# Block sums of an output weight spread over more slabs, and more weight buffers in the output projection, in a one-core hybrid decoder layer

## Chip, core and metric

One core of a Trainium2 chip. The metric is device time in microseconds (us) for one execution. The kernel before took 2124.35 us (median of three runs, 2124.03 to 2127.09); the execution that was profiled took 2120.17 us.

## What is computed

A decoder layer on x of 1024 tokens by 2048 channels, in float32:

```
h     = rms_norm(x, attn_norm_g)
proj  = h @ w_in                       # 7776 columns, split into the parts below
q,k,v = silu(causal_conv4(gq, gk, gv)) # 8 heads of 128: group A
o_a   = gated_delta_rule(q, k, v, g, beta);  o_a = rms_norm(o_a) * silu(gz)
I     = sum_h w[t,h] * relu(q_idx[t,h] . k_idx[s])   # indexer, 16 heads of 64
o_b   = softmax attention of each query over its 256 best keys by I, * silu(az)
out   = rms_norm(x + concat(o_a, o_b) @ w_out, final_norm_g)
```

## The kernel before

**Numbers.** Each float32 factor is split into a high part `hi` (rounded by a ScalarE copy) and a rest `lo`, and a product is three matmuls (hi·hi, hi·lo, lo·hi).

**Input projection.** The work is cut into slabs of 256 columns of `w_in`. A slab has 8 pieces (`w_piece`, L198): SyncE (SP) loads the piece into `wraw` (3 buffers, 256 KB), ScalarE (ACT) writes `whi` (L194), GpSimd (POOL) writes `wlo` (L195; 2 buffers each), and TensorE (PE) does 24 matmuls of 512 columns with it (L289). Order of the slabs: V of the attention, a small one, four slabs `iq` of the indexer and the fifth `qk` slab (beside them the indexer's scores, with loads `iqr` at L492), four `qk` slabs (beside them the search for the 256th best score on VectorE, DVE, L661), then `k` 0 to 3 and `q` 0 to 3 of group A with their convolutions (beside them the attention, whose queries are loaded as `qaT`, L810, and whose masks are stored at L690), `v` 0 to 3 (beside them a triangular solve on DVE), and the gates, with the delta rule beside them.

**Output projection.** One level of Strassen's scheme: seven products (i = 0 to 6) of 512 x 1024 x 1024, each as two halves c of 8 pieces k. Four of the seven right factors are sums of 1024 x 1024 blocks of `w_out`. These sums (`wsum`, 4 MB each, in DRAM) are formed by DMA alone: eight steps (copy a block, or add one to it with an accumulating DMA), each cut into 4 parts of R = 256 rows (1 MB), 32 DMAs from POOL's queue. `block_sums` (L1130) puts them into a list `per_piece`; `w_piece` takes one off the list in pieces 1 to 5 of each slab and issues it on POOL right behind that piece's `wlo`. The list holds 17 entries of the delta rule's decay first, so the first `wsum` DMA goes out in the fourth `qk` slab and the last in slab `q` 1.

A piece of the output (`w_out_piece`, L219) loads `wraw` (same 3 buffers), ACT writes `whi` (L228) and DVE writes `wlo` (L229); two pieces of three have their `whi`/`wlo` in pool `wp` (2 buffers), the third in pool `op` (1 buffer). PE does 12 matmuls with it (L1383). At the end of each half `take` (L1319) adds the four PSUM banks to accumulators on DVE, `with_x` (L1301) loads x into a tile `xr` of pool `stage` (4 buffers) and adds it on POOL, and `square` (L1309) has ACT sum the squares, with its unused elementwise output in a small bfloat16 tile `jk` of its own.

**What sets the order.** Every engine and queue works in order. The order is written by a list planner from priorities (weights first, then evictions, side work, matmuls) and a timeline that it simulates, so an instruction that waits holds up all behind it on its engine.

Of the kernel before, what the change touches and what calls it, by code (L numbers as in the profile page):

```python
# [12 lines left out]
F32 = mybir.dt.float32  # L13
F32R = mybir.dt.float32r
BF16 = mybir.dt.bfloat16
I32 = mybir.dt.int32
AF = mybir.ActivationFunctionType
ALU = mybir.AluOpType
# [4 lines left out]
P = 128  # L23
T = 1024
D = 2048
# [14 lines left out]
HT = 512  # L40
# [12 lines left out]
def hybrid_layer(ctx: ExitStack, tc, x, positions, attn_norm_g, w_in, conv_w, a_log, dt_bias,  # L53
                 gdn_g, w_out, final_g, out):
    nc = tc.nc
    V, S, G, PE, SP = nc.vector, nc.scalar, nc.gpsimd, nc.tensor, nc.sync
# [3 lines left out]
    w_out = w_out[0]  # L60
# [5 lines left out]
    @contextmanager  # L66
    def pri(base):
        if active[0] == base:
            yield
            return  # L70
        saved = tc.cur_priority, active[0]
        tc.cur_priority, active[0] = count.get(base, base), base
        yield
        count[base] = tc.cur_priority
        tc.cur_priority, active[0] = saved
# [5 lines left out]
    wp = ctx.enter_context(tc.tile_pool(name="wp", bufs=3))  # L81
    gp = ctx.enter_context(tc.tile_pool(name="gp", bufs=1))
    stage = ctx.enter_context(tc.tile_pool(name="stage", bufs=2, side="right"))
    dr = ctx.enter_context(tc.tile_pool(name="dr", bufs=1, space=DRAM))
# [42 lines left out]
    def after(ins, prev):  # L127

        tc.add_manual_dep(ins.ins, prev.ins.name,
                          mybir.DependencyInfo(mybir.DependencyClass.NoSync, mybir.DependencyReason.DATA), reason="order")  # L130
        return ins
# [57 lines left out]
    w0 = w0_cm.__enter__()  # L189

    per_piece = []

    def w_split(whi, wlo, raw, ncol, eng):
        ins = S.activation(whi[:, :, :ncol], raw[:, :, :ncol], AF.Copy)  # L194
        low = eng.tensor_tensor(wlo[:, :, :ncol], raw[:, :, :ncol], whi[:, :, :ncol].bitcast(F32), op=ALU.subtract)  # L195
        return ins, low

    def w_piece(srcs, p, ncol, w2d, keep=False, into=None):  # L198

        with pri(P_W):  # L200
            raw = wp.tile([P, KPP, CG], F32, tag="wraw", name="wraw")
            o = 0
            for c0, n in srcs:
                SP.dma_start(raw[:, :, o:o + n], w2d[p * KPP * P:(p + 1) * KPP * P, c0:c0 + n].rearrange("(k p) c -> p k c", p=P))
                o += n
            if into is not None:
                whi, wlo = into
            elif keep and p >= 2:
                whi = w0.tile([P, KPP, CG], F32R, name=f"whi0_{p}")
                wlo = w0.tile([P, KPP, CG], F32R, name=f"wlo0_{p}")  # L210
            else:
                whi = wp.tile([P, KPP, CG], F32R, tag="whi", name="whi", bufs=2)
                wlo = wp.tile([P, KPP, CG], F32R, tag="wlo", name="wlo", bufs=2)
            ins = w_split(whi, wlo, raw, ncol, G)
            if per_piece and 1 <= p <= 5:
                per_piece.pop(0)(*ins)
        return whi, wlo

    def w_out_piece(src):  # L219

        with pri(P_W):
            shape = [P, 2 * CG]
            raw = wp.tile(shape, F32, tag="wraw", name="wraw")
            SP.dma_start(raw, src)
            pool, bufs = (op, 1) if next(turn_k) % 3 == 2 else (wp, 2)
            whi = pool.tile(shape, F32R, tag="whi", name="whi", bufs=bufs)
            wlo = pool.tile(shape, F32R, tag="wlo", name="wlo", bufs=bufs)
            S.activation(whi, raw, AF.Copy)  # L228
            V.tensor_tensor(wlo, raw, whi.bitcast(F32), op=ALU.subtract)  # L229
        return whi, wlo  # L230
# [344 lines left out]
    with tc.tile_pool(name="dp", bufs=1, reuse_waits="tile") as dp, pri(P_SIDE):  # L575
# [3 lines left out]
        r = dp.tile([P, NB, HEADS], F32, name="drr")  # L579
# [30 lines left out]
    early_cm.__exit__(None, None, None)  # L610


    maskS = [dr.tile([P, (b + 1) * P], BF16, name=f"mask{b}") for b in range(NB)]
    with tc.tile_pool(name="scp", bufs=1, reuse_waits="tile") as scp:
        score = {b: scp.tile([P, (b + 1) * P], F32, name=f"score{b}") for b in range(2, NB)}
        with ExitStack() as ixs:
            ixk = ixs.enter_context(tc.tile_pool(name="ixk", bufs=1, reuse_waits="tile"))
            kst = [ixk.tile([P, T], F32R, name=f"kst{i}") for i in range(2)]
            wi = ixk.tile([P, NB, 16], F32, name="wi")
            with pri(P_SIDE):  # L620
                V.tensor_scalar(wi, sm[:, :, 0:16], 0.03125, None, op0=ALU.mult)
                with tc.tile_pool(name="ikp", bufs=1, reuse_waits="tile") as ikp:
                    raw = ikp.tile([P, T], F32, name="ikr")
                    for i in range(2):
                        SP.dma_start(raw[64 * i:64 * i + 64], ikT)
                    S.activation(kst[0], raw, AF.Copy)
                    V.tensor_tensor(kst[1], raw, kst[0].bitcast(F32), op=ALU.subtract)
            ixp = ixs.enter_context(tc.tile_pool(name="ixp", bufs=1, reuse_waits="tile"))

            for cslab in range(4):  # L630
                iq_slab(cslab)
            proj_qk(4, budget=float("inf"))
# [6 lines left out]
        with tc.tile_pool(name="tkp", bufs=1, reuse_waits="tile") as tkp, pri(P_SIDE):  # L639
# [40 lines left out]
            for i in reversed(range(NK)):  # L680
                b, n = blocks[i], (blocks[i] + 1) * P
# [247 lines left out]
    def part(c, q):  # L929
        return (q * NB + c) * HEADS  # L930
# [70 lines left out]
    def delta_rule(g2):  # L1001
        def t4(tag, bufs):
            return g2.tile([P, 4, P], F32, tag=tag, name=tag, bufs=bufs)
# [53 lines left out]
        def step(c, ld, St, last):  # L1057
            G2 = range(2)
            pa = [mm4("pa", ld[g]["kT"], St[g]) for g in G2]
            prepare(c, ld)  # L1060
            R = []
            for g in G2:
                R.append(t4("R", 2))
                for h in range(4):
                    V.scalar_tensor_tensor(R[g][:, h, :], pa[g][:, h, :], col(cg, c, g, h), ld[g]["vb"][:, h, :],
                                           op0=ALU.mult, op1=ALU.add)
            pv = [mm4("pv", ld[g]["TT"], R[g]) for g in G2]
            vn = []
# [50 lines left out]
            SP.dma_start(szT[:, i0 + g, h * HT:(h + 1) * HT], sz[:, 3:])  # L1119
        slab_cm([(c0, CG)], CG, ev, budget=budget)  # L1120


    HC = D // 2

    def wo(i, j):
        return w_out[(1 - i) * HC:(2 - i) * HC, j * HC:(j + 1) * HC]

    wsum = {n: dr.tile([HC, HC], F32, name=f"wsum{n}") for n in (1, 2, 3, 4)}

    def block_sums():  # L1130

        R = 256

        def part(dst, src, add, r):
            def fn(ins, low):
                sl = slice(r * R, (r + 1) * R)
                ld = G.dma_start(wsum[dst][sl], src[sl], accum_op=ALU.add) if add else G.dma_start(wsum[dst][sl], src[sl])
                after(ld, low)
            return fn
        for dst, src, add in ((1, wo(0, 0), False), (3, wo(0, 1), False), (1, wo(0, 1), True), (3, wo(1, 1), True),  # L1140
                              (2, wsum[1], False), (2, wo(1, 1), True), (4, wsum[2], False), (4, wo(1, 0), True)):
            for r in range(HC // R):
                per_piece.append(part(dst, src, add, r))

    def decay_units():

        E = {}
# [33 lines left out]
        proj_qk(c)  # L1181
    tabs_cm.__exit__(None, None, None)
    with tc.tile_pool(name="atp", bufs=1, reuse_waits="tile") as atp:
        block_sums()
        attention(atp, kvp)
        total = sum(w for w, _ in todo)
        slabs = [("k", i) for i in range(4)] + [("q", i) for i in range(4)]
        for n, (nm, i) in enumerate(slabs):
            proj_conv(nm, {"k": C_GK, "q": C_GQ}[nm] + i * CG, 2 * i,
                      budget=float("inf") if n == NSLAB - 1 else total / NSLAB)  # L1190
            if n == 4:
                with pri(P_SIDE):
                    V.tensor_scalar(ssk, ssk, 4 * EPS, None, op0=ALU.add)
                    rsqrt(gp, rk.rearrange("p b h -> p (b h)"), ssk.rearrange("p b h -> p (b h)"), NU)
                    V.tensor_tensor(vs, rk, beta, op=ALU.mult)
                    V.tensor_tensor(cg, cn, egc, op=ALU.mult)
                    V.tensor_scalar(vs, vs, 0.5, None, op0=ALU.mult)
# [32 lines left out]
    op = ctx.enter_context(tc.tile_pool(name="op", bufs=1, reuse_waits="tile"))  # L1230
    turn_k = itertools.count()
# [6 lines left out]
    pairs = [[bigt(f"pr{i}{q}", [P, NT, 2, HT], F32R) for q in range(2)] for i in range(2)]  # L1238
    acc = [bigt(f"acc{i}", [P, NT, HC]) for i in range(2)]
    y11 = bigt("y11", [P, NT, HC])  # L1240
    m22 = bigt("m22", [P, KH, HT])
# [59 lines left out]
    def with_x(hf, ch, j, cs, sub=False):  # L1301

        xr = stage.tile([P, 3 + HT], F32, tag="xr", name="ox", bufs=4)[:, 3:]
        t0 = hf * HT + j * P
        SP.dma_start(xr, x[t0:t0 + P, ch * HC + cs.start:ch * HC + cs.stop])
        y = ys[hf, ch][:, j, cs]
        G.tensor_tensor(y, y, xr, op=ALU.subtract if sub else ALU.add)

    def square(hf, ch, j, c):  # L1309
        cs = slice(c * 512, (c + 1) * 512)  # L1310
        jk = op.tile([P, 512], BF16, tag="jk", name="jk", bufs=1)
        n = 2 * ch + c
        S.activation(jk, ys[hf, ch][:, j, cs], AF.Square, accum_out=ss[:, NT * hf + j, n:n + 1])

# [132 lines left out]
```

## Time and profile before

| | |
|---|---|
| median of the runs | 2124.35 us |
| profiled execution | 2120.17 us, span 2118.5 us |
| PE busy | 2030.4 us (96%) |
| DVE / ACT / POOL busy | 1350.0 / 882.0 / 685.2 us |
| mean granted clock of TensorE | 0.991 |
| DMA bytes | 285.59 MB, mean 135 GB/s |

Busy times are sums over a span; PE busy close to the span means that the kernel's time is PE's work plus the gaps in it. The granted clock is 1.00 where the full 2.4 GHz is granted; lower values in a stretch mean that part of it ran at 1.2 GHz.

### The profile page before, as it was taken

The page shows a single profiled execution, that of the slowest core. Times are in us where ns is not written, and L with a number is a line of the kernel's source. Part 1 is how long each engine was busy: PE and PEld are TensorE (multiplying, and loading weights), DVE is VectorE, ACT ScalarE, POOL GpSimd, SP SyncE. Part 2 cuts the span into 40 slices and gives each one's busy share as a digit, 9 for nine tenths or more (in the row PEclk, how much of TensorE's full clock was granted, in tenths as well). Part 3 has the DMA queues.
Part 4 walks back from the last instruction along what each step waited for, and adds up shares of the span by engine and source line. Part 5 has one row for each costly group of instructions (what it writes and reads, how often), then busy time and mean ns, then how long its engine had stood idle before and what let it go on. Part 6 is the DMA issues. An engine that isn't in the chain of part 4 may idle for free.

```text
span 2118.5 us, 29832 instructions
## 1 busy us (share of the span) xinstructions
PE 2030.4 (96%) x10145; PEld 1702.0 (80%) x10145; DVE 1350.0 (64%) x2830; ACT 882.0 (42%) x2070; POOL 685.2 (32%) x660
## 2 busy tenths in 40 slices
PE   7999999999999789999999999899999999999997
PEld 6888888877887677888888887778889888778776
DVE  7625766899999555645555548990254416478766
ACT  7424544433223355444554542212355523333335
POOL 5434344555553212222221112232232221014441
PEclk9999999999999999999999999999999999999999
DMA  6222232344368876655222223227666437655435
GB/s 188 74 69 79 78 85 75 106 121 126 107 191 195 208 207 158 175 128 125 88 73 64 69 72 90 80 70 185 183 178 189 132 119 258 215 177 166 156 117 219
DMA packets 278057, 285.59 MB, mean 135 GB/s; under 512 B 67168, under 2 KB 213008, under 8 KB 277200
## 3 DMA queue, kind: packets, MB, share of 16 engines
q1 hardware_dynamic: 227920, 221.81, 35.0%
q0 software_dynamic: 6784, 33.56, 7.0%
q10 hardware_dynamic: 43200, 28.32, 4.6%
q8 instruction: 80, 1.31, 0.3%
q14 instruction: 73, 0.60, 0.1%
HBM read 217.12 MB, written 100.04 MB: 150 GB/s over the span
## 4 chain that ended last, share of the span: by engine, by line
PE 47%; DVE 10%; DMA 8%; issue 1%; ACT 1%; SPq 1%; ACTq 0%; POOL 0%; DVEq 0%
PE cm L289 25%; PE to L1383 10%; DVE ut L944 3%; DVE mb L946 2%; PE po L148 2%; PE lgp L148 2%; DMA pr<-szT 2%; DMA qaT<-qkT 2%; PE pT L151 1%; DMA mask<-mk 1%; DVE wlo L229 1%; DVE pr L1264 1%; DVE cy L711 1%; PE pv L920 1%; PE hh L920 1%
## 5 line engine op out<-in xcount | busy, mean ns | idle before, releaser
L289 PE MATMUL cm<-hT,whi 128*128 128x512 f32 (+1 forms) x3776 | 1206.6, 395 | 7.2 <-DVE sz L1118 6.3
L289 PEld LDWEIGHTS cm<-hT,whi 128*128 128x128 f32 (+1 forms) x3776 | 705.6, 188 | 151.4 <-DVE sz L1118 7.6
L289 PE MATMUL cm<-hT,wlo 128*128 128x512 f32 (+1 forms) x1888 | 744.7, 394 | 8.5 <-POOL wlo L195 8.4
L195 POOL TENSOR_TENSOR wlo<-wraw,whi 128x512 fp32r<-128x512 f32 (+1 forms) x248 | 339.3, 1369 | 888.7 <-ACT whi L194 864.6
L289 PEld LDWEIGHTS cm<-hT,wlo 128*128 128x128 f32 (+1 forms) x1888 | 355.3, 188 | 84.3 <-POOL wlo L195 13.2
L194 ACT ACTIVATE whi<-wraw 128x512 fp32r<-128x512 f32 (+1 forms) x248 | 153.6, 619 | 338.4 <-PE cm L289 236.4
L1383 PE MATMUL to<-whi,pr 128*128 128x512 f32 x832 | 257.5, 391 | 1.8 <-DVE sz L1118 1.2
L661 DVE TENSOR_SCALAR_CACHE_REDUCE tj<-score,cand 128x384 bf16<-128x384 f32 (+2 forms) x198 | 187.2, 945 | 6.4
L1383 PEld LDWEIGHTS to<-whi,pr 128*128 128x128 f32 x832 | 156.1, 188 | 36.4 <-DVE sz L1118 1.6
L1383 PE MATMUL to<-wlo,pr 128*128 128x512 f32 x416 | 163.2, 395 | 9.6 <-DVE wlo L229 9.6
L516 DVE SCALAR_TENSOR_TENSOR score<-rl,wi,score 128x512 f32<-128x512 f32 (+3 forms) x150 | 127.4, 858 | 30.1 <-ACT rl L508 23.5
L711 DVE SCALAR_TENSOR_TENSOR cy<-xr,convw,cy 128x512 f32<-128x512 f32 x144 | 123.1, 855 | 19.8 <-ACT cy L709 18.4
L229 DVE TENSOR_TENSOR wlo<-wraw,whi 128x512 fp32r<-128x512 f32 x104 | 94.4, 917 | 59.6 <-ACT whi L228 59.4
L228 ACT ACTIVATE whi<-wraw 128x512 fp32r<-128x512 f32 x104 | 64.6, 626 | 100.3 <-PE to L1383 58.5
L829 DVE CUSTOM_DVE_ANT_0 lg<-lgp,mk 128x512 f32<-128x512 f32 (+3 forms) x96 | 53.1, 554 | 80.4 <-PE lgp L148 80.1
L1383 PEld LDWEIGHTS to<-wlo,pr 128*128 128x128 f32 x416 | 78.1, 188 | 31.9 <-DVE wlo L229 14.7
L508 ACT ACTIVATE rl<-isc 128x512 f32<-128x512 f32 (+1 forms) x105 | 58.9, 571 | 55.5 <-PE isc L148 31.1
L848 DVE TENSOR_TENSOR pT<-pT 128x512 fp32r<-128x512 f32 (+1 forms) x80 | 49.6, 633 | 50.3 <-ACT pT L847 49.8
L1118 DVE SCALAR_TENSOR_TENSOR sz<-sz,cm 128x512 f32<-128x512 f32 x32 | 21.6, 682 | 93.3 <-ACT sz L1117 93.3
L148 PE MATMUL lgp<-kT,qaT 128*128 128x512 f32 (+3 forms) x288 | 70.0, 351 | 4.2 <-DVE mx L829 4.2
L713 ACT ACTIVATE xr<-cy 128x512 f32<-128x512 f32 x48 | 30.3, 631 | 103.5 <-DVE cy L711 90.2
L148 PE MATMUL po<-pT,vv 128*128 128x256 f32 x432 | 72.7, 288 | 0.0
(301 smaller groups left out, 2727.1 us busy)
## 6 DMA issues: line engine op xcount, KB each, us to landing
wraw<-in_w_in_dram SPq DMA_DIRECT2D x232, 256.0 KB, 2.9
wsum<-in_w_out_dram POOLq DMA_DIRECT2D x24, 1024.0 KB, 11.1
wraw<-wsum SPq DMA_DIRECT2D x64, 256.0 KB, 2.9
wraw<-in_w_out_dram SPq DMA_DIRECT2D x48, 256.0 KB, 3.3
xt<-in_x_dram SPq DMA_DIRECT2D x32, 256.0 KB, 3.7
szT<-sz SPq DMA_DIRECT2D x32, 256.0 KB, 3.0
pr<-oT SPq DMA_DIRECT2D x32, 256.0 KB, 5.3
pr<-szT SPq DMA_DIRECT2D x32, 256.0 KB, 5.4
```

Of the source, the lines that this page charges most:

```text
L148: return anchored(PE.matmul(*a, **k))
L194: ins = S.activation(whi[:, :, :ncol], raw[:, :, :ncol], AF.Copy)
L195: low = eng.tensor_tensor(wlo[:, :, :ncol], raw[:, :, :ncol], whi[:, :, :ncol].bitcast(F32), op=ALU.subtract)
L228: S.activation(whi, raw, AF.Copy)
L229: V.tensor_tensor(wlo, raw, whi.bitcast(F32), op=ALU.subtract)
L289: mms.append(PE.matmul(bank[:n, :], w[:, k, g * P:g * P + n], h_ap(kt, a, slice(h * HT, h * HT + HT)), start=(p == 0 and k == 0 and i == 0 ...
L508: S.activation(rl[:, :w], ps2[:, :w], AF.Relu)
L516: V.scalar_tensor_tensor(dst, r, w1, dst, op0=ALU.mult, op1=ALU.add)
L661: V.tensor_scalar(junk[:, :(b + 1) * P], score[b], cand[:, i:i + 1], 0.0, op0=op, op1=ALU.add, accum_out=cnt[:, i:i + 1])
L711: V.scalar_tensor_tensor(y, xr[:, j:j + HT], convw[:, j, ch:ch + 1], y, op0=ALU.mult, op1=ALU.add)
L944: V.tensor_tensor(tv, u[:, j + 1:, j:j + 1].to_broadcast([P, n, j]), u[:, j:j + 1, :j].to_broadcast([P, n, j]), op=ALU.mult)
L1383: PE.matmul(banks[j], a[:, j * P:(j + 1) * P], w, start=(k == first and n == 0), stop=(k == last and n == 2))
```

## The change

The parts of the block sums have 128 rows (512 KB) in place of 256, so there are 64. They go into a list of their own, `per_other`, which is filled before the first `iq` slab; `w_piece` takes one in pieces 0, 2, 4 and 6 of a slab when `per_piece` is empty. In `w_out_piece` the pieces take turns between `wp` and `op`, with two buffers of `whi` and `wlo` in each. `jk` is now a tile of the rotation `xr` in `stage`, in float32.

```
+    per_other = []
...
             if per_piece and 1 <= p <= 5:
                 per_piece.pop(0)(*ins)
+            if per_other and not per_piece and p % 2 == 0:
+                per_other.pop(0)(*ins)
...
-            pool, bufs = (op, 1) if next(turn_k) % 3 == 2 else (wp, 2)
-            whi = pool.tile(shape, F32R, tag="whi", name="whi", bufs=bufs)
-            wlo = pool.tile(shape, F32R, tag="wlo", name="wlo", bufs=bufs)
+            pool = op if next(turn_k) % 2 else wp
+            whi = pool.tile(shape, F32R, tag="whi", name="whi", bufs=2)
+            wlo = pool.tile(shape, F32R, tag="wlo", name="wlo", bufs=2)
...
     def block_sums():
-        R = 256
+        R = P
...
-                per_piece.append(part(dst, src, add, r))
+                per_other.append(part(dst, src, add, r))
...
+            block_sums()
             for cslab in range(4):
                 iq_slab(cslab)
...
     with tc.tile_pool(name="atp", bufs=1, reuse_waits="tile") as atp:
-        block_sums()
         attention(atp, kvp)
...
     def square(hf, ch, j, c):
-        jk = op.tile([P, 512], BF16, tag="jk", name="jk", bufs=1)
+        jk = stage.tile([P, 3 + HT], F32, tag="xr", name="jk", bufs=4)[:, 3:]
```

## Rows read from the trace of the kernel before

**Rows 1.** Windows: stretch, length, busy time (count) per engine, clock, DMA share, GB/s
```profile
100.00:400.00 300.00, 298.63 (x1358) 247.08 (x1357) 174.48 (x254) 133.89 (x244) 121.80 (x107) 1.00 0.28 77
400.00:660.00 260.00, 254.78 (x1131) 209.14 (x1130) 249.78 (x555) 80.55 (x190) 140.01 (x135) 1.00 0.52 146
660.00:870.00 210.00, 180.54 (x928) 151.08 (x927) 130.07 (x309) 92.84 (x273) 51.73 (x58) 0.94 0.76 188
870.00:1250.00 380.00, 380.00 (x2015) 322.59 (x2015) 210.94 (x522) 189.72 (x497) 81.57 (x94) 1.00 0.35 94
1750.00:2107.00 357.00, 345.54 (x1496) 279.07 (x1494) 243.58 (x371) 141.43 (x259) 99.16 (x65) 1.00 0.54 182
```
**Rows 2.** Timeline of TensorE's weight loads, 690 to 870 us, behind their longest waits
```profile
714.87 0.71 PEld L151 LDWEIGHTS ctok<-ident,xr 128*128 128x128 f32 x4 [10.77 <-DVE gce L733]
...
753.11 1.14 PEld L151 LDWEIGHTS pT<-ident,lg 128*128 128x128 f32 x6 [8.59 <-DVE lg L837]
...
840.66 0.82 PEld L148 LDWEIGHTS lgp<-kT,qaT 128*128 128x128 f32 x3 [4.65 <-DVE mx L829]
```
**Rows 3.** Timeline of VectorE, 655 to 765 us: the wait for a mask store
```profile
711.37 0.49 DVE L688 TENSOR_SCALAR mk<-score,cand 128x512 bf16<-128x512 f32 x1 [8.24 <-DMA mask<-mk]
```
**Rows 4.** Timeline of ScalarE, 655 to 842 us: its waits for DMAs
```profile
699.11 0.64 ACT L713 ACTIVATE xr<-cy 128x512 f32<-128x512 f32 x1 [7.26 <-DMA Md<-gce]
...
749.00 0.42 ACT L811 ACTIVATE qaT<-qaT 128x256 fp32r<-128x256 f32 x1 [6.89 <-DMA qaT<-qkT]
```
**Rows 5.** Chain that ended last, in order of time: start, length of the piece
```profile
694.22 18.78 DMA mask<-mk
...
737.45 11.52 DMA qaT<-qkT
...
825.81 13.29 DMA qaT<-qkT
```
**Rows 6.** Timeline of GpSimd, 590 to 960 us: block-sum DMAs issued
```profile
682.95 0.87 POOL L1137 DMA_DIRECT2D wsum<-in_w_out_dram  x1
...
691.00 1.11 POOL L1137 DMA_DIRECT2D wsum<-in_w_out_dram  x1
...
736.91 0.87 POOL L1137 DMA_DIRECT2D wsum<-in_w_out_dram  x1
```
**Rows 7.** DMA issues: count, KB each, median us to landing; then line L1137
```profile
wsum<-in_w_out_dram POOLq DMA_DIRECT2D x24, 1024.0 KB, 11.1
wraw<-wsum SPq DMA_DIRECT2D x64, 256.0 KB, 2.9
...
qaT<-qkT SPq DMA_DIRECT2D x32, 128.0 KB, 2.6
...
L1137 POOL DMA_DIRECT2D wsum<-in_w_out_dram x24: 572/864/1109, 577.8 to 966.9; - x24
```
**Rows 8.** Windows of 10 us, columns as before: two stalls, two stretches without
```profile
710.00:720.00 10.00, 5.13 (x19) 4.33 (x20) 6.11 (x15) 3.64 (x14) 1.34 (x1) 0.62 0.75 192
750.00:760.00 10.00, 6.69 (x30) 6.11 (x31) 7.86 (x22) 6.74 (x22) 0.18 (x1) 0.57 0.34 106
890.00:900.00 10.00, 10.00 (x59) 8.76 (x58) 7.81 (x14) 6.60 (x19) 3.79 (x6) 1.00 0.84 284
920.00:930.00 10.00, 10.00 (x59) 8.67 (x59) 2.30 (x6) 4.41 (x14) 3.38 (x3) 1.00 1.02 186
```
**Rows 9.** Waits, whole span: engine, line, waited for, us in total, times, longest
```profile
POOL wlo L195 <- ACT whi L194: 864.6, 186, 14.2
...
ACT qT L494 <- DMA iqr<-iqT: 39.3, 12, 7.3
```
**Rows 10.** Waits within 1765 to 2118 us, of PE, ACT and the SP queue
```profile
PE to L1383 <- DVE wlo L229: 9.6, 9, 2.5
...
ACT whi L228 <- PE to L1383: 58.5, 24, 6.5
...
SPq L1305 <- POOL acc L1307: 17.5, 12, 4.0
```

More of the change, by code (lines that the diff above doesn't have):

```diff
@@ L610, in hybrid_layer, with wo, block_sums, part @@
     early_cm.__exit__(None, None, None)
+    HC = D // 2
+    def wo(i, j):
+        return w_out[(1 - i) * HC:(2 - i) * HC, j * HC:(j + 1) * HC]
+    wsum = {n: dr.tile([HC, HC], F32, name=f"wsum{n}") for n in (1, 2, 3, 4)}
+    def block_sums():
+        R = P
+        def part(dst, src, add, r):
+            def fn(ins, low):
+                sl = slice(r * R, (r + 1) * R)
+                ld = G.dma_start(wsum[dst][sl], src[sl], accum_op=ALU.add) if add else G.dma_start(wsum[dst][sl], src[sl])
+                after(ld, low)
+            return fn
+        for dst, src, add in ((1, wo(0, 0), False), (3, wo(0, 1), False), (1, wo(0, 1), True), (3, wo(1, 1), True),
+                              (2, wsum[1], False), (2, wo(1, 1), True), (4, wsum[2], False), (4, wo(1, 0), True)):
+            for r in range(HC // R):
+                per_other.append(part(dst, src, add, r))
     maskS = [dr.tile([P, (b + 1) * P], BF16, name=f"mask{b}") for b in range(NB)]
@@ L1120, in proj_gate @@
         slab_cm([(c0, CG)], CG, ev, budget=budget)
[L1123 to L1130, printed above, removed]
-        R = 256
[L1134 to L1142, printed above, removed]
-                per_piece.append(part(dst, src, add, r))
     def decay_units():
```

## The prediction

> **What bounds the kernel now.** I read the page's busy times first: PE is busy 2030.4 of 2118.5 us, so the time is PE's work plus some 88 us of gaps, and the change alters no matmul. The question is which gaps it closes or opens. The windows by stage show where they are [rows 1]: PE busy 298.63 of 300 us in the indexer's stage, 254.78 of 260 beside the search for the 256th score, 180.54 of 210 from 660 to 870, 380.00 of 380 after that, 345.54 of 357 in the output projection. So 29.5 us of gap lie in one stretch, the only one of the five with a mean clock under 1.00 (0.94), at the highest DMA share (0.76); 11.5 us lie in the output projection. The rest (start, solve, tail) has nothing that the change touches.
>
> The timeline of weight loads names the gaps of the stretch: 10.77, 8.59 and 4.65 us, behind DVE each time [rows 2]. DVE itself was waiting: 8.24 us for a mask store to land [rows 3]; and in the second case ACT waited 6.89 us for a query load, DVE being next in that line [rows 4]. The chain of waits shows these DMAs taking 18.78, 11.52 and 13.29 us [rows 5], where the median query load lands in 2.6 us [rows 7]. GpSimd's timeline gives the reason [rows 6]: three block-sum DMAs of 1 MB went out from 682.95 to 691.00 (first and last shown), 3 to 11 us ahead of the mask store, and another at 736.91, half a microsecond ahead of the query load. Their median landing is 11.1 us [rows 7]. Three of them from 682.95 to the mask's landing at 713.00 are 30 us, 10 us each: a small DMA that starts behind them shares the engines until they are through.
>
> **Block sums, spread and halved.** Per slab, 4 parts of 512 KB (2 MB) in place of 5 of 1 MB. The first 20 go out in the four `iq` slabs and the fifth `qk` slab, 3 in the fourth of the later `qk` slabs (the 17 decay entries end in its piece 2), 32 in `k` and `q`, 9 in `v`. 64 in all, the last some 300 us before the output projection reads them.
>
> Removed, the mask stall: with parts of 5 us each (half of 10), issued at most one per two pieces (8 to 16 us here), the queue ahead of a store is at most 5 us and not 30. The store issued at 694.22 then lands before 703.13, when DVE came to wait (711.37 less 8.24), and the 8.24 us go [rows 3]. Of PE's 10.77 us I take 8.2, the other 2.5 being DVE's own work. ACT's 7.26 us behind the `Md` store just before [rows 4] cost PE some 1.5 us more. Term: -9.7, bounds 0 and -12.5.
> Removed, the query stalls: a load that meets one half part lands in about 2.6 + 5 = 7.6 us in place of 11.5 to 13.3, so ACT's wait falls from 6.89 to about 3, and such a meeting comes about only where a load falls into the 5 us after an issue (every 20 us in a slab of 80 us, one time in four). Of 8.59 + 4.65 = 13.2 us I take -10, and -1.5 for smaller gaps of the kind. Bounds 0 and -15.
> Clock: in the windows of 10 us behind the stalls the granted clock fell to 0.62 and 0.57 [rows 8]; it fell after PE had stood still for some 9 to 11 us. Busy time by one less the clock gives 5.13 x 0.38 + 6.69 x 0.43 = 4.8 us for two of them, with smaller losses beside them. Where the stalls go, so does that: -5, bounds 0 and -7.
>
> Added, meetings in the indexer's stage. The DMAs most exposed are its 24 pairs of `iqr` loads, which ACT waits for in order, with the weight split and the score eviction behind it. With a part of 5 us every 14 us (a slab of 57 us), one pair in three, 8, meets one, for 2.5 us on average: 20 us more of ACT's waits. ACT waits 39.3 us for them now, up to 7.3 us at a time [rows 9], while PE loses 1.4 us in the whole stage [rows 1]: its weights are a piece ahead, and POOL idles 864.6 us over the kernel for ACT to bring more [rows 9]. The cover ends at a wait of about 10 us. Term: +3, bounds 0 and +34 (the rival below).
> Added, meetings from 970 to 1450 us, where there were no block sums. Those from 870 to 967 are the nearest rows: with 1 MB parts in flight and DMA shares of 0.84 and 1.02 PE stays busy 10.00 of 10 us [rows 8]. Term: +1, bounds 0 and +5.
> POOL's issue time: 64 x 0.57 to 0.86 us (the least and the median of a 1 MB issue, [rows 7]) is 37 to 55 us against some 23 now. It stands behind a `wlo` and ahead of the next, for which POOL waits 4.6 us on average (864.6 / 186, [rows 9]). Term: 0; without that cover +32 at most.
>
> The Trainium skill's page "DMA: Bandwidth & Descriptors", section "Bandwidth", speaks against the halving: it wants batches of at least 1 MiB and gives each DMA about 2 us that do not shrink with size. By it 32 more DMAs are 64 us more of queue time, an estimate from that page. No run here shows a block sum of 512 KB yet, and the sum above uses half of the measured 10 us.
>
> **Four buffers in the output projection.** PE waits 9.6 us in 9 places for `wlo`, and ACT waits 58.5 us in 24 places for PE to free a `whi` [rows 10]. With a fourth buffer ACT and DVE can be one piece further ahead, 12 matmuls of 0.231 us (345.54 / 1496, [rows 1]) or 2.8 us; the longest of PE's waits is 2.5 us. Where DVE is busy without a break the piece ahead is no earlier, so I take -7, bounds 0 and -11.5 (all gaps of the stage). What is late next is `wraw` with its 3 buffers, loaded in 2.9 us [rows 7] against 2.8 us of PE per piece and three pieces of cover.
> `jk` in the rotation `xr`: in product 2 the x loads and the squares alternate, so an x load waits for the addition two loads back and not four, and SP holds the weight loads behind it. SP waits 17.5 us there now, 4.0 us at most [rows 10]; the three buffers of `wraw` cover 8 us. Term: +1, bounds 0 and +16. The tile's wider type costs nothing that I can see: an ACT instruction that writes float32 of that size takes 0.64 us [rows 4]. No work lies on the one extra wait of ACT, since a square follows the addition that frees its buffer.
>
> **Sum.** -9.7 - 11.5 - 5 + 3 + 1 + 0 - 7 + 1 = -27 us. Against the profiled execution, 2120.17 us, that is 2093; the median of the runs, 2124.35, lies 4.2 us above it, and I put the change on that: 2097 us.
>
> **Rivals.**
> 1. *Halving doesn't shorten a part* (10 us each as now, only spread). Then meetings outside the bunched one cost as before: -9.7 and some 3 us of clock, -7, +4 for the two kinds of added meetings, +1: about -12 to -15, 2111 us. For it: nothing shows how the 11.1 us split into a fixed part and bytes. Against it: 10 us per MB three in a row look like bytes. Chance 0.13.
> 2. *The x loads hold SP.* Per half of products 2 and 4 four takes need POOL some 3 us each, 12 us against 8 us of cover, so 4 us of PE per half, 16 over four halves in place of +1: -12, 2112 us. Against it: POOL's share of PE's gaps there is nothing so far. Chance 0.10.
> 3. *The stalls only move.* DVE is busy 249.78 of 260 us up to 660 [rows 1] and the planner writes a new order for every engine; its backlog then stands where the mask stood, and the loss of 29 us stays but for the bunched DMAs' clock: -4 to +4, 2124 us. For it: 2.5 of the 10.77 us were DVE's own. Against it: DVE is idle for 80 of the 210 us after 660 [rows 1]. Chance 0.11.
> 4. *Slower: the indexer's stage pays.* A meeting there costs PE what one costs in `k` 1 to 3: 4.65 to 8.59 us for a whole part [rows 2], so up to 4.3 for a half. 8 meetings are 34 us, and the clock that falls behind such gaps some 8 more, in place of +3: -27 + 39 = +12, 2136 us. It decides from 3.4 us per meeting (27 / 8). For it: PE works in order, and ACT's waits of 7.3 us are already at the cover's edge. Against it: they cost 1.4 us in all. Chance 0.13.
>
> **How the numbers follow.** The forecast has 0.53, the rivals 0.13, 0.10, 0.11 and 0.13. A measurement of this kernel tells 0.2%, 4.2 us, from no change. The forecast and rivals 1 and 2 are faster by more (0.76, less 0.02 for what planning may cost), rival 3 is mostly within it, rival 4 beyond it: 0.74, 0.11, 0.15. All gaps of the two stretches and the clock together are 29.5 + 11.5 + 5 = 46 us, so 2080 is near the floor; 2128 takes in rivals 1 to 3 and leaves out the most of rival 4. The forecast's own range is 2085 to 2108.
>
> **What would show it.** Right: from 660 to 870 us PE's gaps fall from 29 to under 12 us, no clock under 0.8 in any 10 us there, block-sum DMAs landing in about 5 to 6 us, no wait for `mask` on DVE; `wlo` at L229 gone from PE's waits but for some 2 us. Wrong: landings of 9 us or more (rival 1); SP waiting over 30 us at L1305 (rival 2); the same gaps behind DVE's own work (rival 3); gaps of PE over 10 us between 150 and 400 us behind ACT's wait for `iqr` (rival 4). A time over 2128 us would make the prediction wrong as a whole.

## The result and the profile after

The kernel after takes 2106.1 us (median of four runs, 2105.54 to 2108.41) against 2125.72 us for the kernel before on the same chip: a ratio of 0.9909, 95% interval 0.9892 to 0.9926, which is 19.6 us less (15.7 to 23.0). The forecast was 2097 us, 27 us less, in a range of 2080 to 2128: the direction and the range held, and 2106 lies near the upper end of the forecast's own range of 2085 to 2108; the gain that was forecast was 7 us too large.

The profiled execution took 2106.55 us (span 2104.8). PE is busy 2033.8 us, 3.4 us more than before, so the gaps (the span less PE's busy time) went from 88.1 to 71.0 us. The windows by stage (stretch, length, busy time and count of PE, PEld, DVE, ACT and POOL, granted clock, DMA share, GB/s) answer to [rows 1]; the last one lies as far from the span's end as the last one there:

```profile
100.00:400.00 300.00, 295.64 (x1335) 243.80 (x1334) 169.31 (x248) 131.57 (x241) 128.99 (x122) 0.99 0.42 110
400.00:660.00 260.00, 253.98 (x1124) 208.00 (x1123) 249.60 (x541) 79.66 (x180) 144.71 (x141) 1.00 0.49 128
660.00:870.00 210.00, 199.45 (x1043) 166.35 (x1042) 146.23 (x373) 103.44 (x309) 50.98 (x58) 0.99 0.57 152
870.00:1250.00 380.00, 380.00 (x2011) 322.13 (x2010) 207.34 (x493) 191.53 (x489) 90.84 (x114) 1.00 0.39 103
1250.00:1450.00 200.00, 186.29 (x835) 152.02 (x834) 156.78 (x163) 50.51 (x98) 54.50 (x43) 0.97 0.36 99
1450.00:1740.00 290.00, 284.73 (x1704) 250.39 (x1703) 99.15 (x337) 122.42 (x334) 78.85 (x84) 1.00 0.56 158
1736.00:2093.00 357.00, 351.09 (x1521) 284.71 (x1520) 239.79 (x377) 141.08 (x260) 95.73 (x66) 1.00 0.56 187
```

In the stretch of the stalls, 660 to 870 us, PE's gap fell from 29.5 to 10.6 us and the clock rose from 0.94 to 0.99. PE does 1043 matmuls there, 115 more than before; at 0.189 us each (380.00 / 2015 in [rows 1], a stretch without gaps) that is, by estimate, 21.7 us gained. The output projection's gap fell from 11.5 to 5.9 us. The indexer's stage lost 3.0 us (gap 1.4 to 4.4). Two stretches that the prediction gave no row for lost time too; these are their windows before:

```profile
1250.00:1450.00 200.00, 188.31 (x846) 153.58 (x845) 160.50 (x174) 54.98 (x105) 58.63 (x49) 0.98 0.34 94
1450.00:1740.00 290.00, 288.93 (x1742) 254.94 (x1741) 99.00 (x338) 124.09 (x339) 78.88 (x83) 1.00 0.56 161
```

Beside the triangular solve the gap grew from 11.7 to 13.7 us, beside the delta rule from 1.1 to 5.3 (how much of this is the change's own is taken up below).

The windows of 10 us of the kernel after, two of them those of [rows 8], and two more with the largest gaps that are left:

```profile
670.00:680.00 10.00, 7.94 (x36) 6.22 (x35) 10.00 (x21) 1.86 (x3) 1.74 (x2) 0.95 0.35 62
...
710.00:720.00 10.00, 9.66 (x46) 7.49 (x45) 3.87 (x11) 3.67 (x14) 1.74 (x2) 1.00 0.58 161
720.00:730.00 10.00, 7.15 (x32) 4.96 (x31) 4.67 (x13) 4.88 (x9) 2.97 (x3) 1.00 0.80 232
...
750.00:760.00 10.00, 9.56 (x55) 8.15 (x56) 9.27 (x21) 8.33 (x28) 3.20 (x4) 1.00 0.56 147
```

Where PE was busy 5.13 and 6.69 of 10 us at a clock of 0.62 and 0.57, it is now busy 9.66 and 9.56 at 1.00. In the timeline of weight loads the two longest waits up to 715 us are short beside those of [rows 2], and the first stands behind DVE at its own work (DVE is busy 10.00 of 10 us there):

```profile
677.66 0.42 PEld L151 LDWEIGHTS ctok<-ident,xr 128*128 128x128 f32 x4 [2.48 <-DVE gce L760]
...
691.26 0.19 PEld L292 LDWEIGHTS cm<-hT,wlo 128*128 128x128 f32 x1 [1.71 <-POOL wlo L196]
```

DMA issues (count, KB each, median us to landing) answer to [rows 7]:

```profile
wsum<-in_w_out_dram POOLq DMA_DIRECT2D x48, 512.0 KB, 6.2
...
wsum<-wsum POOLq DMA_DIRECT2D x16, 512.0 KB, 4.8
...
qaT<-qkT SPq DMA_DIRECT2D x32, 128.0 KB, 2.7
```

A part of half the size lands in 6.2 us in place of 11.1. DVE waits for no `mask` store any more; the slowest of those lands in 4.0 us, where the slowest before took 21.8.

Waits over the whole span (engine, line, waited for, us in total, times, longest), the two loads that ACT waits for; then the waits in the output projection, which answer to [rows 10]:

```profile
ACT qaT L838 <- DMA qaT<-qkT: 36.8, 24, 5.0
ACT qT L497 <- DMA iqr<-iqT: 34.6, 13, 6.0
```
```profile
SPq L1308 <- POOL acc L1310: 10.1, 9, 1.7
...
PE to L1386 <- DVE sz L1145: 3.3, 1, 3.3
PE to L1386 <- DVE wlo L232: 2.1, 3, 0.9
```

ACT's longest wait for a query is 5.0 us (7.6 before), and its waits for `iqr` did not grow (39.3 before). PE waits 2.1 us for `wlo` where it waited 9.6, and what is late next is not `wraw` but the last gate's `sz` at the start of the stage. SP is held less than before, not more.

### The profile page after: what moved, and what is told of

Its sections match the earlier page's. It is cut to its first block, busy times and chain, and to the rows that moved or that the text cites. A ratio compares the mean times of both kernels' runs of the same rounds, so it can differ in the third digit from the quotient of the medians.

```text
span 2104.8 us, 29853 instructions
## 1 busy us (share of the span) xinstructions
PE 2033.8 (97%) x10145; PEld 1702.9 (81%) x10145; DVE 1348.9 (64%) x2830; ACT 881.6 (42%) x2070; POOL 696.9 (33%) x692
## 4 chain that ended last, share of the span: by engine, by line
PE 48%; DVE 10%; DMA 5%; issue 2%; ACT 1%; SPq 1%; POOL 0%; ACTq 0%; DVEq 0%; POOLq 0%
PE cm L292 24%; PE to L1386 13%; DVE ut L971 3%; DVE mb L973 3%; PE po L148 2%; PE lgp L148 2%; PE pT L151 1%; DVE cy L738 1%; PE ctok L151 1%; DMA gcd<-gcrow 1%; PE hh L947 1%; DMA qaT<-qkT 1%; PE pv L947 1%; DMA mb<-Md 1%; DMA mt<-ms 0%
## 5 line engine op out<-in xcount | busy, mean ns | idle before, releaser
L292 PEld LDWEIGHTS cm<-hT,wlo 128*128 128x128 f32 (+1 forms) x1888 | 355.8, 188 | 85.8 <-POOL wlo L196 13.7
L738 DVE SCALAR_TENSOR_TENSOR cy<-xr,convw,cy 128x512 f32<-128x512 f32 x144 | 121.9, 847 | 24.8 <-ACT cy L736 23.4
L232 DVE TENSOR_TENSOR wlo<-wraw,whi 128x512 fp32r<-128x512 f32 x104 | 88.2, 855 | 59.2 <-ACT whi L231 59.1
L1145 DVE SCALAR_TENSOR_TENSOR sz<-sz,cm 128x512 f32<-128x512 f32 x32 | 21.7, 682 | 85.0 <-ACT sz L1144 84.9
L1092 DVE SCALAR_TENSOR_TENSOR R<-pa,cg,vb 128x128 f32<-128x128 f32 x64 | 17.9, 344 | 89.9 <-PE pa L947 89.9
L971 DVE TENSOR_TENSOR ut<-mb 128x62 f32<-128x62 f32 (+30 forms) x62 | 67.2, 1084 | 10.6 <-DMA mb<-Md 8.9
```

Source lines behind the costliest of these rows:

```text
L292: mms.append(PE.matmul(bank[:n, :], w[:, k, g * P:g * P + n], h_ap(kt, a, slice(h * HT, h * HT + HT)), start=(p == 0 and k == 0 and i == 0 ...
L738: V.scalar_tensor_tensor(y, xr[:, j:j + HT], convw[:, j, ch:ch + 1], y, op0=ALU.mult, op1=ALU.add)
L971: V.tensor_tensor(tv, u[:, j + 1:, j:j + 1].to_broadcast([P, n, j]), u[:, j:j + 1, :j].to_broadcast([P, n, j]), op=ALU.mult)
```

## Experiments

Each kernel was timed against the kernel before on the same chip. A minus is time gained. "Gap" is the length of a stretch less PE's busy time there, from a profiled execution of that kernel. A fence that begins with a stretch of time shows windows by stage of the kernel just measured, columns as above; of other fences the sentence ahead says what they are.

**One part of the change at a time.** The kernel after with the old output projection (the buffer choice and `jk` as before):

```
-            pool = op if next(turn_k) % 2 else wp
+            pool, bufs = (op, 1) if next(turn_k) % 3 == 2 else (wp, 2)
...
-        jk = stage.tile([P, 3 + HT], F32, tag="xr", name="jk", bufs=4)[:, 3:]
+        jk = op.tile([P, 512], BF16, tag="jk", name="jk", bufs=1)
```

> The new block sums alone (128 rows, own list, from the first indexer slab on); the output projection as before. Contention theory: from 660 to 870 us PE's gaps fall from 29.5 to about 11 us and the clock stays up, the indexer's stage pays about 3 us; in all 16 to 20 us faster than before, about 2107 us. Rival, that the gain comes from the output projection's buffers: under 6 us faster, 2120 us or more. Rival, that the planner's new order made it: the time lands anywhere, and the gaps of 660 to 870 us need not go.

Measured: 2113.48 us, ratio 0.9928 [0.9906, 0.9951], which is -15.3 us (-10.4 to -20.0).

```profile
660.00:870.00 210.00, 199.56 (x1040) 166.81 (x1038) 145.54 (x368) 104.15 (x311) 50.19 (x58) 0.98 0.56 151
```

That is just under the 16 us that were expected at least. The stretch is as in the kernel after (gap 10.4), and PE's wait for `wlo` in the output projection stays at 9.7 us.

The kernel before with the new output projection alone:

```
-            pool, bufs = (op, 1) if next(turn_k) % 3 == 2 else (wp, 2)
+            pool = op if next(turn_k) % 2 else wp
...
+        jk = stage.tile([P, 3 + HT], F32, tag="xr", name="jk", bufs=4)[:, 3:]
```

> Four buffers and jk in the rotation xr alone; block sums as before. Contention theory: only PE's waits for wlo in the output projection go (9.6 us before), 4 to 7 us faster, about 2120 us, and the gaps from 660 to 870 us stay near 29 us. Rival (order): those gaps change by more than 5 us though no block sum was touched. Rival (x loads hold SP): no gain or a loss, SP's wait for the x loads over 30 us.

Measured: 2119.66 us, 0.9969 [0.9953, 0.9986], -6.6 us (-3.0 to -10.0).

```profile
660.00:870.00 210.00, 182.06 (x925) 152.12 (x924) 130.73 (x310) 93.00 (x272) 49.97 (x58) 0.93 0.77 191
...
1450.00:1740.00 290.00, 286.70 (x1723) 252.38 (x1722) 97.50 (x336) 122.11 (x335) 77.48 (x82) 0.99 0.56 160
```

DVE's wait for the mask store is there too:

```profile
DVE mk L688 <- DMA mask<-mk: 10.2, 1, 10.2
```

The stalls are all there (gap 27.9), and PE's wait for `wlo` falls to 2.0 us. The two parts add up within their intervals: -15.3 and -6.6 are -21.9, against -19.6 measured together.

The kernel before with `jk` in the rotation `xr` and the old weight buffers:

> The kernel before with jk in the rotation xr and nothing else. If the x loads then hold SP: 2 us or more slower than before, SP's waits at the x loads above 25 us. If not: within 2 us of before, and what the output projection gained is the buffers'. A change of over 4 us with no change in SP's waits would be the planner's order alone.

Measured: 2128.60 us, 1.0010 [0.9993, 1.0027]: no difference that can be told. SP waits somewhat less than before ([rows 10] has 17.5 us, 12 times), as its waits in the output projection show:

```profile
SPq L1305 <- POOL acc L1307: 13.6, 8, 3.8
```

PE's wait for `wlo` stays at 9.4 us. So the move of `jk` costs nothing that can be told, and the -6.6 us of e2 go with the fourth buffer, as the wait for `wlo` does. Rival 2 falls. The stretch beside the delta rule, long before `jk` is used, is needed below:

```profile
1450.00:1740.00 290.00, 283.68 (x1718) 249.91 (x1717) 100.42 (x336) 122.12 (x336) 77.44 (x82) 1.00 0.57 161
```

**Size, place and rate of the block sums.** The kernel after with parts of 1 MB at the same bytes per slab, and the old output projection, so that against e1 the size alone differs:

```
-        R = P
+        R = 256
...
-            if per_other and not per_piece and p % 2 == 0:
+            if per_other and not per_piece and p % 4 == 0:
```

> As the first, but parts of 256 rows (1 MB), taken in pieces 0 and 4 of a slab: the same bytes per slab, not halved. If the halving matters as forecast: a part takes some 10 us to land, the mask stall is gone but single queries and index loads still meet 10 us, so 10 to 14 us faster than before, 2112 to 2116 us. If only the spreading matters: as the first, within 3 us (about 2107).

Measured: 2121.67 us, 0.9972 [0.9956, 0.9988], -6.0 us.

```profile
660.00:870.00 210.00, 196.49 (x1020) 164.90 (x1019) 140.57 (x357) 101.53 (x300) 47.11 (x54) 0.98 0.55 149
...
1450.00:1740.00 290.00, 279.58 (x1680) 245.21 (x1679) 98.64 (x335) 119.89 (x332) 77.37 (x82) 1.00 0.54 156
```

The 10 to 14 us that were expected did not come. At equal bytes per slab the kernel with halves (e1) is some 9 us faster (0.9972 - 0.9928), but only 3.1 us of that lie in the stretch (gap 13.5 against 10.4). The largest part lies beside the delta rule (gap 10.4 against 4.6 in e1), where no block sum is issued any more (the last goes out at 1180.8 us) and where e4 below loses as much without any; that part is not shown to be the halving's. Whole parts landing in 9.8 us cost the indexer's stage nothing (its gap is 0.3 us), so what rival 4 feared does not come from the parts' length.

The kernel before with halves alone: the list, the place and one part per piece stay as they were, so a slab carries 2.5 MB in place of 5:

```
-        R = 256
+        R = P
```

> The kernel before with parts of 128 rows and nothing else: 64 parts of 512 KB from the old place and by the old rule (pieces 1 to 5), so 2.5 MB per slab in place of 5 and no part in the indexer's stage. If parts of 5 us at half the rate are what takes the stalls away: the gaps from 660 to 870 us near 12 us and 12 to 16 us faster than before, about 2112 us, as the new block sums alone. If the early start is needed: gaps above 18 us there, under 8 us faster.

Measured: 2105.43 us, 0.9901 [0.9881, 0.9921], -21.1 us (-16.8 to -25.3).

```profile
660.00:870.00 210.00, 203.63 (x1077) 171.18 (x1076) 148.38 (x371) 107.94 (x312) 53.67 (x67) 0.99 0.64 162
```

One changed constant gives at least what all the new block sums give, and more than the 12 to 16 us expected. The gap is 6.4 us, less than in the kernel after. But e4 below, with no block sum at all, gains only 14.7 us, so not all of the 21.1 us can be traffic taken away; the largest difference between the two is the gap beside the delta rule, 2.7 us here and 10.7 there.

ACT's waits for a query, in the kernel before and in e5:

```profile
ACT qaT L811 <- DMA qaT<-qkT: 48.0, 24, 7.6
...
ACT qaT L811 <- DMA qaT<-qkT: 48.7, 23, 5.5
```

Over the whole span their sum is the same, and yet the gap from 660 to 870 us went from 29.5 to 6.4 us: what PE loses does not follow the sum of these waits.

Halves, but two of them back to back in a piece, so that place and rate are those of the kernel before:

```
+            if per_other and not per_piece and 1 <= p <= 5:
+                per_other.pop(0)(*ins)
+                per_other.pop(0)(*ins)
...
+        R = P
```

> The kernel before with parts of 128 rows, two of them issued back to back in each piece: the bytes per piece and slab as before, only the DMAs are shorter. If what counts is how much is queued ahead of another DMA: the gaps from 660 to 870 us stay above 22 us and no more than 6 us are gained. If the length of one DMA counts: gaps near 12 us and 15 us or more faster, as with single halves.

Measured: 2139.63 us, 1.0069 [1.0047, 1.0091], 14.7 us slower than before.

```profile
660.00:870.00 210.00, 178.70 (x893) 148.16 (x892) 124.38 (x300) 91.07 (x269) 59.65 (x72) 0.93 0.76 187
```

Its DMA issues (count, KB, median us to landing), and behind them the one of DVE's two waits for a `mask` store that is longest, from its timeline:

```profile
wsum<-in_w_out_dram POOLq DMA_DIRECT2D x48, 512.0 KB, 8.5
```
```profile
707.89 0.92 DVE L692 TENSOR_SCALAR mk<-score,cand 128x384 bf16<-128x384 f32 x1 [4.15 <-DMA mask<-mk]
```

The stalls are back (gap 31.3), down to DVE's wait for a `mask` store, and a half now takes 8.5 us to land. So it is not the size of one DMA that makes the stalls, but how many bytes stand queued ahead of a small DMA. Why this kernel is 14.7 us slower than the one before is not settled: its gap in the stretch is 1.8 us larger, and beside the delta rule, where no block sum is issued any more (the last at 971.3 us), it is 7.7 us (1.1 in the kernel before, 6.3 in e7).

Whole parts, in three pieces of five (3 MB per slab), at the old place:

```
+            if per_other and not per_piece and p in (1, 3, 5):
+                per_other.pop(0)(*ins)
```

> The kernel before with whole parts of 1 MB in pieces 1, 3 and 5 only: 3 MB per slab in place of 5, from the old place on. If what counts is how much is queued ahead: no bunch of three any more but still 10 us ahead of single loads, gaps from 660 to 870 us of 13 to 20 us, 8 to 14 us faster than before. If the rate alone counts: as the halved parts at 2.5 MB per slab, 18 us or more faster.

Measured: 2129.32 us, 1.0004 [0.9991, 1.0017]: nothing gained, where 8 to 14 us were expected.

```profile
660.00:870.00 210.00, 192.85 (x982) 161.00 (x981) 134.50 (x336) 99.62 (x293) 48.27 (x53) 0.96 0.67 162
...
1450.00:1740.00 290.00, 279.14 (x1687) 245.17 (x1687) 99.45 (x336) 120.72 (x334) 77.04 (x82) 1.00 0.55 157
```

The chain of waits of the same kernel, start and length of the piece:

```profile
811.16 8.95 DMA qaT<-qkT
...
830.95 10.49 DMA qaT<-qkT
```

The lower rate takes 12 us of gap out of the stretch, and DVE waits for no `mask` store any more, though a query load that meets a whole part still takes 9 to 10 us in the chain; 10 us come back beside the delta rule, behind the last block sum (1211.1 us). At nearly the same rate (2.5 MB per slab) halves gained 21 us: 10.8 us of the difference lie in the stretch (gap 17.2 against 6.4), 8.2 beside the delta rule, where e4 below loses as much without any block sum.

Parts of 256 KB in every piece, in the kernel after:

```
-        R = P
+        R = P // 2
...
-            if per_other and not per_piece and p % 2 == 0:
+            if per_other and not per_piece:
```

> The kernel after with parts of 64 rows (256 KB), one in each piece of a slab: the same bytes per slab in smaller parts. If the length of a part is what other DMAs pay: landings near 3 us, and up to 3 us faster than after (2103). If what is left is no longer contention: within 2 us of after. If each part costs POOL its issue (128 x 0.6 us): POOL over 30 us busier and PE's waits for wlo longer, 3 us or more slower.

Measured: 2104.60 us, 0.9897 [0.9874, 0.9920], not to be told from the kernel after. Its DMA issues:

```profile
wsum<-in_w_out_dram POOLq DMA_DIRECT2D x96, 256.0 KB, 4.5
```

ACT's waits for a query are shorter still, but the gap from 660 to 870 us stays (10.5 us; 10.6 in the kernel after), so these waits can hardly be what still costs PE there:

```profile
ACT qaT L838 <- DMA qaT<-qkT: 26.1, 23, 2.8
```

128 issues in place of 32 raise POOL's busy time from 685.2 to 733.9 us and cost nothing that can be seen: the forecast's 0 for POOL holds.

**What the block sums cost at all, and the early start.** The kernel before without block sums; the output projection reads blocks of `w_out` in their place, so the amount of work on PE, DVE and ACT stays, and POOL has 32 DMAs less to issue:

```
-        block_sums()
...
-    RIGHT = (wo(0, 0), wsum[3], wo(1, 0), wsum[2], wsum[1], wo(1, 1), wsum[4])
+    RIGHT = (wo(0, 0), wo(0, 1), wo(1, 0), wo(0, 0), wo(0, 1), wo(1, 1), wo(1, 0))
```

> The kernel before without the block sums: the output projection reads blocks of w_out in the place of the sums, so the output is another one. It bounds what contention can cost. Contention theory: the gaps from 660 to 870 us fall under 10 us and the kernel is 20 to 26 us faster than before, about 2102 us, that is 2 to 6 us better than the new block sums alone. Rival (DVE's backlog takes the place of the DMAs): gaps of 20 us or more stay from 660 to 870 us, and under 10 us are gained.

Measured: 2112.41 us, 0.9931 [0.9907, 0.9955], -14.7 us, where 20 to 26 were expected.

```profile
660.00:870.00 210.00, 201.69 (x1059) 170.32 (x1058) 149.26 (x366) 107.29 (x308) 44.34 (x51) 0.98 0.45 123
...
1450.00:1740.00 290.00, 279.27 (x1667) 244.37 (x1666) 100.28 (x336) 120.12 (x331) 77.42 (x82) 1.00 0.54 155
```

With no block sum at all a gap of 8.3 us stays in the stretch, so most of the 10.6 us of the kernel after are not the block sums' (8.3 is no strict floor: e5 has 6.4, and e9 below, with the same order up to the output projection, 8.9). Beside the delta rule this kernel has a gap of 10.7 us, the largest but one of all, with no block sum anywhere. So a loss of that size there needs no traffic of theirs.

The kernel after with its list filled behind the search and not ahead of the first `iq` slab (`block_sums()` moved down to where it stood before):

> The kernel after with its list filled behind the search instead of ahead of the indexer: no block sums in the indexer's stage, the parts run on into the gates' slabs. If the meetings in the indexer's stage cost what they seem to (4.4 us of gap from 100 to 400 us against 1.4), these 3 us come back: about 2103 us. If those gaps are only the planner's order: within 2 us of the kernel after (2106), or worse where the parts now meet the loads of the delta rule (2108 to 2112).

Measured: 2114.97 us, 0.9948 [0.9930, 0.9966], -11.1 us.

```profile
660.00:870.00 210.00, 201.54 (x1051) 169.35 (x1050) 146.12 (x364) 105.68 (x308) 52.56 (x64) 0.98 0.58 154
```

The longest of PE's waits for a DMA from 1250 to 1740 us, and the load behind it in the chain of waits (start and length):

```profile
PE x L1002 <- DMA P1bd<-Ps: 4.7, 1, 4.7
...
1446.23 2.97 DMA P1bd<-Ps
```

The indexer's stage is free of its loss (gap 1.3 us) and the stretch is as good, but from 1250 to 1740 us the gaps come to 24.8 us (19.0 in the kernel after), with that wait for a load of the solve's among them. The load landed 2.97 us after its start (the median of its kind in this kernel is 3.2), so it was issued late rather than held up by a part. The kernel is slower than either forecast of its time.

**The best of both.** e5 with the new output projection, beside the kernel after once more:

> The kernel before with parts of 128 rows at the old place and by the old rule, and the new output projection (four buffers, jk in xr). If the two gains add (21 and 6.6 us): about 2100 us, 26 to 28 us faster than before and some 5 better than the kernel after. If the halved parts' time of 2105 us came from a lucky order: 2105 us or more, no better than after.

Measured: 2100.20 us, 0.9878 [0.9860, 0.9897], -26.0 us.

```profile
660.00:870.00 210.00, 201.13 (x1071) 168.74 (x1070) 147.28 (x368) 107.05 (x309) 54.52 (x66) 1.00 0.63 160
```

> The kernel after once more, beside the three others on the same chip. Every theory: 17 to 21 us faster than before. Its gaps from 1450 to 1740 us tell whether the 4 us that its first profile shows above the kernel before are the change's (again 5 us or more) or vary between executions of one order.

Measured: 2110.42 us, 0.9925 [0.9908, 0.9942], just under the 17 us expected at least, and 10.2 us above e9 on the same chip.

```profile
100.00:400.00 300.00, 296.07 (x1337) 244.28 (x1336) 170.78 (x249) 132.20 (x241) 129.40 (x122) 0.99 0.42 110
...
1450.00:1740.00 290.00, 285.76 (x1703) 251.41 (x1702) 99.53 (x337) 121.33 (x333) 79.37 (x84) 0.99 0.55 158
```

The second profile of the kernel after repeats the first: gaps of 3.9 and 4.2 us in these two stretches. The kernel with two of the edits (`R = P` and the output projection) and without the new list beats both kernels.

## Why the prediction came out as it did

**The place and the mechanism were right.** The mask stall went: no wait for `mask`, no clock under 0.8 in any 10 us from 660 to 870 (the lowest is 0.88), a gap under the 12 us that were named as the mark. DVE's wait for a mask store is 8.2, 10.2 and 11.1 us in the three kernels with the old block sums (before, e2, e7), 6.4 in two waits in e10, and 1.1 or less in all others. e10 shows the cause from the other side: the same bytes at the same places in smaller DMAs bring the stall back. Halves land in 6.2 us where 5 to 6 were forecast and 9 would have spoken for rival 1, which falls.

**Smaller DMAs were slower per byte, and that did not matter.** 1 MB in 11.1 us is 94 GB/s, 512 KB in 6.2 us 85, 256 KB in 4.5 us 58; and all landings laid end to end grew (24 x 11.1 + 8 x 6.1 = 315 us before, where the copies within `wsum` land in 6.1; 48 x 6.2 + 16 x 4.8 = 374 after). But nothing waits for a block sum (the last goes out at 1175.8 us, the first is read at 1810.9), and what waits is the small load behind it. The Trainium skill's page "DMA: Bandwidth & Descriptors", section "Bandwidth", asks for batches of at least 1 MiB: of the rate the trace agrees with it; of the kernel's time e5 goes against it and is 21.1 us faster, so for this kernel the measurement decides otherwise. The prediction's estimate from that page, 64 us more of queue time, came out near (374 less 315 is 59 us), and nothing shows that it cost time.

**The term that was mis-sized is the sum of the block sums: -22 forecast, -15.3 measured (e1).** Three terms of it:
- The mask, the query stalls and the clock, -9.7 - 11.5 - 5 = -26.2, measured 21.7 us of PE's work in the stretch. The gap fell by 18.9 us where 21.2 were forecast. Of the 10.6 us left, 4.2 lie from 670 to 700, where DVE is busy 10.00 of 10 (one wait of 2.48 us stands behind DVE; that the rest is DVE's backlog is argued), and 4.6 from 720 to 740, where the attention starts. e4 shows that 8.3 us of gap stay without any block sum, where the two bounds (-12.5 and -15) had left 2.
- The clock by itself, -5: the other 2.8 of the 21.7 us. In the stretch PE spends 199.45 / 1043 = 0.191 us per matmul against 180.54 / 928 = 0.195 before, and some of it is lost elsewhere (a clock of 0.97 in the solve's stretch, 0.98 before). Over the span PE's busy time did not fall at all (2030.4 to 2033.8).
- What the sum had no term for: 6.2 us of gaps more from 1250 to 1740 us, where the forecast had the +1 for added meetings (bound +5) and nothing behind 1450.

**The later loss is in part scatter, and the rest is not settled.** It need not be traffic of block sums, since e4 has a larger one without any. The kernel before, e2 and e7 have the same order of instructions on PE up to the output projection, and so have the kernel after, e1 and e12. Beside the delta rule the gap is 1.1, 3.3 and 6.3 us in the first three and 5.3, 4.6 and 4.2 in the others: on average 3.6 and 4.7. Beside the solve it is 11.7, 12.1 and 10.7 against 13.7, 15.5 and 12.8. So of the 6.2 us some 3.6 are left, most of them beside the solve. The gap of 1.1 was a low one, as was the profiled 2120.17 us, below every median of the kernel before measured here (2125.72 to 2128.05); this is also why the two profiles lie 13.6 us apart and the medians 19.6. The 3.6 us may be the order: each edit of the block sums has the planner write a new one for every engine, and in e6 a wait of 4.7 us for a load issued late stands alone in the solve. A run of one order with another's block sums would tell, and was not tried. For the same reason no more than the gain in the stretch is shown to be the block sums' doing; there the gap is 29.5, 27.9 and 31.8 us in the first three and 10.6, 10.4 and 9.9 in the others.

**The indexer's +3 was right in size and not in reason.** The gap grew by 3.0 us (from 1.4 to 4.4; 3.9 in the second profile), but ACT's waits for `iqr` fell by 4.7 us where they were to grow by 20. PE waits 3.5 us, in two places, for ACT to evict a score (`isc` behind `rl`). Whole parts in the same stage (e3) leave a gap of 0.3, so this too is more likely the order than the traffic; that is argued and not shown. Rival 4's 39 us are out of reach.

**The output projection was right.** -7 + 1 forecast, -6.6 measured (e2), and by the wait that was named: `wlo` from 9.6 to 2.1 us. The +1 for `jk` was nothing (e7).

**Rival 3** has a grain of truth: some 8 of the 29.5 us stay without any block sum (e4); the other two thirds went and did not come back in the stretch.

## What to carry to other kernels

Bulk traffic that nothing waits for is priced by what stands behind it: let one small part stand in the queues at a time, with a gap to the next, and do not issue two in a row. Before building a schedule that spreads such work, try the size of the part alone; here one constant gave at least as much as the new list (it also halves the bytes per slab, since one part goes out per piece). Where a planner rewrites the order after every edit, a stage that the edit does not touch can lose several us, and even with one order its gap can differ by 5 us from one profiled execution to the next (1.1 to 6.3 here); a forecast of 20 us needs a term for that on both sides.

## What the runs showed that had not been expected

- The landing of an accumulating or copying DMA from `w_out` to DRAM is 11.1, 6.2 and 4.5 us for 1 MB, 512 KB and 256 KB: 4.9 us for the second 512 KB, 1.7 us for the second 256 KB, so by estimate from these three a fixed part of some 2 to 3 us lies in the smallest. They come from three kernels whose parts are spaced differently. Copies from `wsum` to `wsum` are faster: 4.8 us for 512 KB.
- Two 512 KB DMAs issued in a row land in 8.5 us each by the median, where single ones land in 6.2 to 6.5, and bring back the gap of one of 1 MB at the same place (31.3 against 29.5 us).
- POOL's busy time grew by 48.7 us for 96 more issues (e8), 0.5 us each, though each carried a quarter of the bytes: the median issue from `w_out` takes POOL 0.76 us for 256 KB and 0.86 for 1 MB. The kernel's time shows no cost of it.
